# PEER mixer of a two-layer diffusion backbone: the order in which token tiles are ranked, and where the gathered expert rows are placed

## The chip, the cores and the metric

The kernel runs on one core of a Trainium2 chip. The metric is the device time of one execution in microseconds (us), the median of the runs. The core has five engines with a queue each: TensorE (PE), VectorE (DVE), ScalarE (ACT), GpSimd (POOL) and SyncE (SP). SP only issues DMAs here; POOL also issues the indirect DMAs that gather rows. Each engine takes its own queue strictly in order.

## The reference, cut to what matters

640 tokens of width 1024 (128 context tokens, 512 latent tokens) pass two layers. Each layer has a sequence mixer and then a channel mixer named PEER. In PEER every token picks 8 heads x 16 experts out of 16384, and each expert is one row of a table u and one row of a table v:

```python
q = (x @ wq).reshape(ntok, 8, 2, 128)
s = einsum('thpk,hpnk->thpn', q, keys)
sv, si = top_k(s, 16)                      # per head, per half of the key
cand = sv[:, :, 0, :, None] + sv[:, :, 1, None, :]
fv, fpos = top_k(cand, 16)                 # 16 of 256 sums
eidx = si0 * 128 + si1 at fpos             # 8 x 16 expert numbers for a token
g = softmax(fv)
act = gelu(einsum('td,ted->te', x, u_tab[eidx]))
out = einsum('te,ted->td', g * act, v_tab[eidx])
```

Everything is float32 at the interface. The two sequence mixers (S5 and RG-LRU in layer 0, Hyena in layer 1) are not touched by the change.

## The kernel before, in words

The 640 tokens are five tiles of 128 tokens. Tile 0 holds the context, tiles 1 to 4 the latents. `peer(l)` runs once in each layer and treats the tiles in two ways. Tiles 0 and 1 are **gathered**: for each of the 128 expert slots of a token, one indirect DMA issued by POOL (L1041) brings 128 rows of 1024 float32, 512 KB, into one of five buffers `gb`. DVE then either multiplies the row with the tokens and sums it (L1053, a "u row") or adds it to `acc` with its weight (L95, a "v row"). One such gather with its DVE operation is called a row below: 128 u rows and then 128 v rows for a tile, 512 rows in each layer, tile 1 first, then tile 0. Tiles 2 to 4 are **dense**: they are multiplied with all 16384 experts, and a gate matrix that holds `g` at the picked experts and zero elsewhere selects.

The stages of `peer(l)` in order of the program:

- Query stage (L1074 to L1122). `proj3` multiplies with `wq` in 16 steps m, two for each head, and `evq` forms the scores of all five tiles at L1101, in the order `ORD`. The first three tiles of `ORD` (slots s = 0, 1, 2 of `ef` and `gt`) are ranked at once: `top16` on DVE, then `stage2`, which sends sums and products to POOL and turns positions into expert numbers `ef`. For slots 1 and 2 (`DECA`) ACT sums the last product (L1014); for slot 0 POOL and DVE do (L1017, L1018). The scores of the fourth and the fifth tile are kept in `sc2` and `sc1`. After each head, `take(it0, BSLOT)` emits BSLOT rows of tile 1. With each m, `tick` emits a part of the matmuls that prepare the modulation vectors (L129).
- Two of the 128 dense up-projections are made ahead (L1149).
- Gate stage (L1362 to L1369). For n = 0, 1, 2, that is tiles 2, 3, 4, `gate_prep(n)` fetches `ef[:, ORD.index(NG + n)]`, and `gate` forms the gate matrix in 16 steps. Each step emits one row (`WSLOT`), whose DVE operation is ordered behind the last `OI` of the step (`behind`). Beside it `late(3, sc2)` ranks the fourth tile of `ORD`, a head for each pair of steps.
- Dense stage (L1254 to L1317 and L1380 to L1391). 128 iterations of 128 experts each: loads of u and v (512 KB each), splits into high and low parts on ACT and DVE, 24 matmuls of the up-projection (L1145), 18 of the down-projection (L1296), and between them gelu and gate. Every eighth iteration loads 1.5 MB of gate matrix `Gt` (L1262). In iterations 0 to 8 `late(4, sc1)` ranks the fifth tile of `ORD`. Rows are emitted as they fall due:

```python
nw = sum(WSLOT[i % len(WSLOT)] for i in range(16 * ND)) + 8 * BSLOT
...
due = min(4 * 128 - nw, (i + 1) * LRATE_N // LRATE_D)
take(it, due - done[0])
```

- Tail: `back` (layer 0) or `final` (layer 1) of the dense tiles, the rest of the rows, and `back` or `final` of tile 0, which needs the last row.

The text of the program is not the order of the queues. The program is built with a scheduler (`schedule_with_timeline_sim=True`) that simulates the instructions and fixes the order in each queue when the kernel is built. The trace shows that order.

The change touches three constants: `ORD` (L926), `BSLOT` (L934) and `LRATE_N` (L956). They act on `evq` (L1100, L1114), `gather` (L1045), `gate_prep` (L1188) and the loop at L1379 to L1391.

Of the kernel before, what the change touches and what calls it, by code (L numbers as in the profile page):

```python
# [43 lines left out]
def tile_kernel(ctx: ExitStack, tc: tile.TileContext, I, O, dbg=None, upto=99):  # L44
# [104 lines left out]
    def tick(n=1):  # L149
        for _ in range(n):  # L150
            if bgm[0] is None or next(bgm[0], False) is False:
                bgm[0] = None
                break
# [769 lines left out]
    g_d = [dram.tile([16, 128, TD // 16, 8, 16], F32, name=f"g_d{l}") for l in range(2)]  # L923

    FG0, FG1 = 6, 3
    ORD = (1, 2, 3, 4, 0)  # L926
    NGB = 5
    NGS = 3
    NRES = 4
# [1 line left out]
    DECH = 8  # L931
    CANDE = G
    WSLOT = (1,)
    BSLOT = 7  # L934
    MTICK = 1
    OIP = (0, 0, 0, 1)
    CT = ((10, 2), (10, 2))
# [15 lines left out]
    MQ = 4  # L953
    MODS_Q = [[(0, (10, 11)), (1, tuple(range(MQ)))], [(1, (10, 11))]]
    VSUB = (0,)
    LRATE_N, LRATE_D = 16, 4  # L956

    def peer(l):
        pool = ExitStack()
# [84 lines left out]
        def gather(i):  # L1044
            s0 = ORD.index(i)  # L1045
            ei = gp.tile([128, 128], I32, name="ei", tag="ei", bufs=2)
            act = gp.tile([128, 128], F32, name="act", tag="act")
            for s in range(128):
                if s % 16 == 0:
                    V.tensor_copy(ei[:, s:s + 16], ef[:, s0, s:s + 16])  # L1050
                b = rows(f"peer_u{l}", ei, s)
                with behind():
                    V.scalar_tensor_tensor(b, b, 1.0, hrow[:, i], op0=ALU.mult, op1=ALU.mult,  # L1053
                                           accum_out=act[:, s:s + 1])
                yield
            w = gp.tile([128, 128], F32, name="pw", tag="pw", bufs=2)
            S.activation(w, act, AF.Gelu_apprx_tanh)
            mul(w, w, gt[:, s0])
            acc = accs[i]
            for s in range(128):  # L1060
                b = rows(f"peer_v{l}", ei, s)
                if s == 0:
                    ts(acc, b, w[:, 0:1], None, ALU.mult, None)
                else:
                    stt(acc, b, w[:, s:s + 1], acc, ALU.mult, ALU.add)
                yield

        def take(it, n):
            for _ in range(n):
                next(it, None)  # L1070
# [3 lines left out]
        with ExitStack() as e0:  # L1074
# [19 lines left out]
            def evq(m, p):  # L1094
# [4 lines left out]
                pb = ps.tile([128, 2, 128], F32, name="psc2", tag="sm2")  # L1099
                for s, i in enumerate(ORD):  # L1100
                    PE.matmul(pa[:, s] if s < 3 else pb[:, s - 3], q[:, i * 128:(i + 1) * 128], keys[:, m],  # L1101
# [10 lines left out]
                if m % 2 == 1:  # L1112
                    stage2(qp, m // 2, 0, 3, v, iu, lambda sh, dt, n: qp.tile(sh, dt, name=n, tag=n, bufs=2))
                    take(it0, BSLOT)  # L1114
                tick(MTICK)
# [71 lines left out]
        def gate_prep(n):  # L1187
            s0 = ORD.index(NG + n)  # L1188
            cd = kp.tile([128, 11, 128], I32, name="cd", tag="Gs", bufs=NGS)
            e32, ij = cd[:, 0], cd[:, 1:3]  # L1190
            ab, fa = (cd[:, 3 + 4 * i:7 + 4 * i].rearrange("p (a b) c -> p a b c", b=2) for i in range(2))
            fa = fa.bitcast(F32)
            V.tensor_copy(e32, ef[:, s0])
            ts(ij[:, 0], e32, 7, None, ALU.logical_shift_right, None)
            ts(ij[:, 1], e32, 127, None, ALU.bitwise_and, None)
            ts(ab[:, 0], ij, 4, None, ALU.logical_shift_right, None)
            ts(ab[:, 1], ij, 15, None, ALU.bitwise_and, None)
            V.tensor_copy(fa, ab)
            ts(fa[:, 0], fa[:, 0], -4.0, None, ALU.add, None)
            ts(fa[:, 1], fa[:, 1], -8.0, None, ALU.add, None)  # L1200
            V.tensor_copy(code[:, 1:3], fa)
            mul(fa, fa, fa)
            stt(code[:, 0], fa[:, 0], -1.0, fa[:, 1], ALU.add, ALU.add)
            nc.sync.dma_start(c_d[l][n], code)
            cr = kp.tile([128, 4, 2, 128], BF16, name="cr", tag="cr", bufs=2)
            nc.sync.dma_start(cr, c_d[l][n].rearrange("(c t) r h k -> (t r) c h k", c=4))
            gT = kp.tile([128, 128], F32, name="gT", tag="gT", bufs=2)
            pt = ps.tile([128, 128], F32, name="pgT", tag="sm")
            PE.transpose(pt, gt[:, s0], ident)
            S.copy(gT, pt)  # L1210
            return cr, gT
# [163 lines left out]
        with ExitStack() as e3:  # L1375
            lp = e3.enter_context(tc.tile_pool(name=f"peerl{l}", bufs=1))
            acc = pp.tile([128, NG, D], F32, name="acc", tag="sc1")
            accs[:] = [acc[:, i] for i in range(NG)]
            nw = sum(WSLOT[i % len(WSLOT)] for i in range(16 * ND)) + 8 * BSLOT  # L1379
            for i, _ in enumerate(dense(lp)):  # L1380
# [366 lines left out]
```

## Time and profile before

| | us |
|---|---|
| median of 3 runs | 4148.82 |
| lowest and highest run | 4145.64, 4162.87 |
| profiled execution, its time | 4159.84 |
| profiled execution, its span | 4158.0 |
| busy in the span: PE, DVE | 3627.4 (87%), 3368.5 (81%) |
| busy in the span: POOL, ACT | 2269.1 (55%), 1708.3 (41%) |

The page of the profile gives busy time by engine, the span in 40 slices, the chain of work that ended last, and the costliest groups of instructions. The views named below are cut out of the same execution: busy time of each engine in chosen stretches, groups by line, waits, the chain in order of time, and the timeline. Times in a view are us from the span's start. A count stands behind an x.

### The profile page before, as it was taken

To read this page: it belongs to the slowest core of one execution; us is meant where nothing else is said; L and a number is where in the kernel's file an instruction comes from. 1 tells how busy PE (TensorE), PEld (TensorE's weight loads), DVE (VectorE), ACT (ScalarE), POOL (GpSimd) and SP (SyncE) were. 2 spreads that over 40 slices of the span, in tenths; PEclk is the share of its full clock that TensorE was granted. 3 is DMA by queue.
4 is the path that set the end of the run, shared out by engine and by line. 5 is a ranking of instruction groups with operands and counts; after the bars stand their busy time and mean duration, and the time that the engine had idled before them with its cause. 6 is when DMAs were issued, how large, how long until landed. Compare 5 with 4: busy or idle time off the path is not lost.

```text
span 4158.0 us, 57343 instructions
## 1 busy us (share of the span) xinstructions
PE 3627.4 (87%) x20098; PEld 3168.2 (76%) x20098; DVE 3368.5 (81%) x6122; ACT 1708.3 (41%) x3493; POOL 2269.1 (55%) x2046
## 2 busy tenths in 40 slices
PE   6867886588999999999689988843889999999996
PEld 4756873467899999999579778742678999999996
DVE  8873599889988887888865656998898888878889
ACT  3522334584333333333354333335843333333333
POOL 5641577658544444455655435886575444444455
PEclk9988998799999999999789999976999999999998
DMA  5565267398999999999724642653989999999997
GB/s 205 138 129 146 87 206 245 119 284 288 358 341 333 347 334 341 340 333 338 246 79 132 222 127 87 209 171 98 287 283 345 343 334 343 335 346 335 335 339 264
DMA packets 438105, 1057.42 MB, mean 254 GB/s; under 512 B 49175, under 2 KB 210967, under 8 KB 432696
## 3 DMA queue, kind: packets, MB, share of 16 engines
q0 software_dynamic: 152784, 555.55, 38.7%
q1 hardware_dynamic: 285032, 498.21, 35.4%
q8 instruction: 158, 2.59, 0.2%
q14 instruction: 131, 1.07, 0.1%
HBM read 993.86 MB, written 61.87 MB: 254 GB/s over the span
## 4 chain that ended last, share of the span: by engine, by line
PE 61%; DVE 22%; DMA 5%; issue 4%; ACT 4%; POOL 3%; SPq 1%; DVEq 0%; ACTq 0%; POOLq 0%
PE pA L1145 24%; PE pso L1296 23%; PE pproj L171 8%; DVE gb L1053 6%; PE pmod L129 1%; DVE oh L77 1%; DMA gb<-in_peer_u,ei 1%; PE pg L1245 1%; DVE OI L1240 1%; POOL gb L1041 1%; ACT Gs L1249 1%; DMA mw<-in_w_mod 1%; DVE tiu L977 1%; POOL jk L77 1%; DVE sc L978 1%
## 5 line engine op out<-in xcount | busy, mean ns | idle before, releaser
L1041 POOL DMA_INDIRECT gb<-in_peer_v,ei x512 | 679.3, 1327 | 627.8 <-DVE acc L95 550.9
L1041 POOL DMA_INDIRECT gb<-in_peer_u,ei x512 | 635.6, 1241 | 527.1 <-DVE gb L1053 401.9
L1296 PE MATMUL pso<-vh,wp 128*128 128x512 f32 x3072 | 874.1, 393 | 5.8 <-ACT wp L1285 4.2
L1053 DVE SCALAR_TENSOR_TENSOR gb<-gb,hrow 128x1024 f32<-128x1024 f32 x512 | 705.8, 1386 | 16.1 <-DMA gb<-in_peer_u,ei 16.1
L1145 PE MATMUL pA<-hHd,ul 128*128 128x384 f32 x2048 | 693.6, 339 | 27.8 <-DVE ul L77 27.8
L1145 PE MATMUL pA<-hHd,uh 128*128 128x384 f32 x2048 | 694.6, 339 | 15.3 <-DVE modT L77 6.7
L1145 PE MATMUL pA<-hLd,uh 128*128 128x384 f32 x2048 | 692.6, 338 | 0.0
L95 DVE SCALAR_TENSOR_TENSOR acc<-gb,pw,acc 128x1024 f32<-128x1024 f32 x508 | 662.0, 1303 | 21.4 <-DMA gb<-in_peer_v,ei 18.0
L1296 PEld LDWEIGHTS pso<-vh,wp 128*128 128x128 f32 x3072 | 574.9, 189 | 114.7 <-ACT wp L1285 5.4
L1137 ACT CAST uh<-wraw 128x1024 fp32r<-128x1024 f32 x256 | 269.2, 1051 | 664.3 <-PE pA L1145 664.2
L77 DVE TENSOR_TENSOR ul<-wraw,uh 128x1024 fp32r<-128x1024 f32 x256 | 318.6, 1244 | 212.1 <-ACT uh L1137 202.8
L1296 PE MATMUL pso<-vl,wp 128*128 128x512 f32 x1536 | 479.4, 393 | 7.5 <-DVE vl L77 7.4
L1145 PEld LDWEIGHTS pA<-hHd,ul 128*128 128x128 f32 x2048 | 389.1, 190 | 30.6 <-DVE ul L77 29.3
L1145 PEld LDWEIGHTS pA<-hHd,uh 128*128 128x128 f32 x2048 | 389.3, 190 | 27.1 <-ACT A L1146 6.9
L1145 PEld LDWEIGHTS pA<-hLd,uh 128*128 128x128 f32 x2048 | 389.1, 190 | 8.7
L1269 ACT CAST vh<-vraw 128x1024 fp32r<-128x1024 f32 x256 | 268.9, 1052 | 243.6 <-PE pso L1296 238.7
L77 DVE TENSOR_TENSOR vl<-vraw,vh 128x1024 fp32r<-128x1024 f32 x256 | 314.5, 1229 | 64.5 <-ACT vh L1269 51.8
L1296 PEld LDWEIGHTS pso<-vl,wp 128*128 128x128 f32 x1536 | 289.5, 189 | 73.6 <-DVE vl L77 9.5
L77 POOL TENSOR_TENSOR wl<-wraw,wh 128x1024 fp32r<-128x1024 f32 (+1 forms) x88 | 215.8, 2454 | 234.7 <-ACT wh L159 211.8
L1285 ACT CAST wp<-A 128x384 fp32r<-128x384 f32 x256 | 131.5, 514 | 428.6 <-DVE A L77 407.1
L1245 PEld LDWEIGHTS pg<-OI,OJ 128*128 128x128 f32 x1536 | 200.9, 202 | 99.7 <-POOL OI L77 34.2
L1245 PE MATMUL pg<-OI,OJ 128*128 128x128 f32 x1536 | 219.5, 292 | 40.9 <-POOL OI L77 16.0
(531 smaller groups left out, 6801.6 us busy)
## 6 DMA issues: line engine op xcount, KB each, us to landing
wraw<-in_uT SPq DMA_DIRECT2D x256, 512.0 KB
vraw<-in_peer_v SPq DMA_DIRECT2D x256, 512.0 KB
g_d<-Gs SPq DMA_DIRECT2D x48, 768.0 KB
Gt<-g_d SPq DMA_DIRECT2D x24, 1536.0 KB
wmod<-in_w_mod SPq DMA_DIRECT2D x48, 512.0 KB
wraw<-in_wq SPq DMA_DIRECT2D x32, 512.0 KB
mw<-in_w_mod SPq DMA_DIRECT2D x16, 1024.0 KB
wraw<-in_w_in_c SPq DMA_DIRECT2D x24, 512.0 KB
```

The source lines that it names most:

```text
L77: (eng or V).tensor_tensor(o, a, b, op=op)
L95: V.scalar_tensor_tensor(o, a, s, b, op0=op0, op1=op1)
L129: PE.matmul(pm[:2, :cw], cond[:, k], w[k], start=k == 0, stop=k == 7)
L171: PE.matmul(p[:, i, :sg[2]], a[:, k, :], sg[hl](k), start=k == 0 and a is wh and hl == 0, stop=k == kk - 1 and a is wl)
L1041: G.indirect_dma_start(out=b, out_offset=None, in_=I[tab], in_offset=bass.IndirectOffsetOnAxis(ap=ei[:, s:s + 1], axis=0))
L1053: V.scalar_tensor_tensor(b, b, 1.0, hrow[:, i], op0=ALU.mult, op1=ALU.mult, accum_out=act[:, s:s + 1])
L1137: S.copy(uh, u)
L1145: PE.matmul(pA, a[:, k], b[:, k], start=k == 0 and b is hHd and a is uh, stop=k == 7 and a is ul)
L1245: PE.matmul(pg[:, t], OJ[:, t4 * 4 + t], OI[:, t4 * 4 + t], start=True, stop=True)
L1269: S.copy(vh, v)
L1285: S.copy(WH, A)
L1296: PE.matmul(pso[n][h], a[:, c], b[:, h * 512:(h + 1) * 512], start=i == 0 and a is WH and b is vh, stop=i == 127 and a is WL)
```

## The change

Three constants differ. The ranking order becomes tiles 2, 3, 4, 1, 0: the three dense tiles are ranked in the query stage, tile 1 by `late(3, sc2)` in the gate stage, tile 0 by `late(4, sc1)` as before. The query stage emits no rows. The rows of the dense stage fall due at 15/4 for an iteration where 16/4 was used; as 48 rows are emitted before the dense stage (104 before the change), 464 are left for it (408 before the change), and they fall due over 124 of 128 iterations (102 before the change).

```diff
@@ -923,7 +923,7 @@
     FG0, FG1 = 6, 3
-    ORD = (1, 2, 3, 4, 0)
+    ORD = (2, 3, 4, 1, 0)
     NGB = 5
@@ -931,7 +931,7 @@
     WSLOT = (1,)
-    BSLOT = 7
+    BSLOT = 0
     MTICK = 1
@@ -953,7 +953,7 @@
     VSUB = (0,)
-    LRATE_N, LRATE_D = 16, 4
+    LRATE_N, LRATE_D = 15, 4
```

## Rows read from the trace of the kernel before

**Rows 1.** The chain that ended last, by line, whole span (page).
```profile
PE pA L1145 24%; PE pso L1296 23%; PE pproj L171 8%; DVE gb L1053 6%; PE pmod L129 1%; DVE oh L77 1%; DMA gb<-in_peer_u,ei 1%; PE pg L1245 1%; DVE OI L1240 1%; POOL gb L1041 1%; ACT Gs L1249 1%; DMA mw<-in_w_mod 1%; DVE tiu L977 1%; POOL jk L77 1%; DVE sc L978 1%
```
**Rows 2.** Busy time by stage: stretch, its length, busy us (count), clock, DMA.
```profile
core 0: us, PE busy (x) PEld busy (x) DVE busy (x) ACT busy (x) POOL busy (x), PEclk, DMA share, GB/s
474.00:780.00 306.00, 221.34 (x1224) 171.75 (x1224) 278.96 (x1040) 130.40 (x649) 220.38 (x272) 0.86 0.55 178
780.00:977.00 197.00, 161.98 (x1019) 127.71 (x1019) 172.72 (x420) 152.17 (x276) 137.29 (x170) 0.93 0.83 258
977.00:2030.00 1053.00, 1047.23 (x5264) 948.85 (x5262) 900.55 (x1095) 376.82 (x507) 547.14 (x421) 1.00 0.93 335
2030.00:2070.00 40.00, 5.83 (x30) 4.00 (x29) 34.27 (x26) 13.63 (x37) 32.54 (x24) 0.56 0.63 195
2553.00:2860.00 307.00, 185.59 (x1068) 162.19 (x1069) 277.51 (x1030) 126.69 (x640) 225.02 (x271) 0.78 0.47 148
...
500.00:520.00 20.00, 20.00 (x136) 18.22 (x135) 19.09 (x114) 8.95 (x42) 13.47 (x20) 1.00 0.13 45
```
**Rows 3.** Tails after the last L1296, 2030.3:2070 and 4120.4:4158: rows and their waiters.
```profile
L95 DVE SCALAR_TENSOR_TENSOR acc<-gb,pw,acc x18: 1271/1284/2932, 2029.6 to 2067.8; 128x1024 f32<-128x1024 f32 x18
...
  PE pac L1166: 27.2, 1
...
L95 DVE SCALAR_TENSOR_TENSOR acc<-gb,pw,acc x13: 1259/1273/2312, 4120.4 to 4145.0; 128x1024 f32<-128x1024 f32 x13
```
**Rows 4.** Gathers alone in parts of the dense stage: DVE busy (x), POOL busy (x).
```profile
1100.00:1800.00 700.00, 311.49 (x379) 325.50 (x251) 1.00 0.94 339
1800.00:2000.00 200.00, 102.45 (x80) 106.65 (x81) 1.00 0.95 337
```
**Rows 5.** Down-projection matmuls alone, L1296, same parts: PE busy (x), PEld busy (x).
```profile
1100.00:1800.00 700.00, 361.25 (x1515) 283.18 (x1513) 1.00 0.94 339
1800.00:2000.00 200.00, 102.98 (x432) 80.85 (x432) 1.00 0.95 337
```
**Rows 6.** Loads of the gate matrix, L1262, in layer 0: first and last issue.
```profile
L1262 SPq DMA_DIRECT2D Gt<-g_d x12: 332/334/892, 1019.3 to 1755.9; - x12
```
**Rows 7.** Rows in the query stage: DVE groups by line, layer 0 (474:780), then layer 1 (2540:2860).
```profile
L1053 DVE SCALAR_TENSOR_TENSOR gb<-gb,hrow 128x1024 f32<-128x1024 f32 x57 | 97.9, 1723 | 3.4 <-DMA gb<-in_peer_u,ei 3.4
...
L1050 DVE CAST ei<-ef 128x16 int32<-128x16 f32 x8 | 6.2, 774 | 0.0
...
L1053 DVE DVE_READ_ACCUMULATOR gb<-gb,hrow 128x1 f32 x57 | 4.3, 76 | 0.0
...
L1053 DVE SCALAR_TENSOR_TENSOR gb<-gb,hrow 128x1024 f32<-128x1024 f32 x56 | 94.2, 1688 | 3.3 <-DMA gb<-in_peer_u,ei 3.3
```
**Rows 8.** The u row by itself, over both layers: min/median/max ns.
```profile
L1053 DVE SCALAR_TENSOR_TENSOR gb<-gb,hrow x512: 1194/1218/7120, 525.5 to 3830.9; 128x1024 f32<-128x1024 f32 x171
```
**Rows 9.** Timeline of POOL, then DVE, 540.65 to 544.2: start, us, engine, operation.
```profile
540.66 2.41 POOL L77 TENSOR_TENSOR wl<-wraw,wh 128x1024 fp32r<-128x1024 f32 x1
...
540.79 3.37 DVE L1053 SCALAR_TENSOR_TENSOR gb<-gb,hrow 128x1024 f32<-128x1024 f32 x1
```
**Rows 10.** Waits, 640:780: who waited for whom, total, times, longest.
```profile
POOL jk L77 <- DVE gb L1053: 21.7, 2, 20.1
```
**Rows 11.** Chain in order of time, 2836:2862, end of layer 1's query stage.
```profile
2836.67 0.79 DVE ef L1018
2837.47 0.07 issue
2837.53 3.28 POOL jk L77 x2
2840.81 7.45 issue
2848.26 0.27 DVE code L1185
...
2858.25 1.01 PE pj L1225 x2
```
**Rows 12.** Timeline of POOL, then DVE, 4113 to 4119.5: gathers issued back to back.
```profile
4113.19 1.36 POOL L1041 DMA_INDIRECT gb<-in_peer_v,ei  x1 [0.30 <-issue]
...
4119.16 0.94 POOL L1041 DMA_INDIRECT gb<-in_peer_v,ei  x1 [0.30 <-issue]
...
4114.12 3.92 DVE L95 SCALAR_TENSOR_TENSOR acc<-gb,pw,acc 128x1024 f32<-128x1024 f32 x3
```
**Rows 13.** Busy time in the 5 us with the highest DMA rate seen, columns as in the stage view.
```profile
531.00:536.00 5.00, 3.79 (x27) 3.53 (x25) 4.69 (x9) 1.70 (x3) 4.70 (x3) 1.00 1.00 382
```

## The prediction, made from the trace of before

> **What bounds the kernel now.** I read the chain that ended last first. Its two largest lines are the dense matmuls, L1145 and L1296, and the u row on DVE (L1053) follows with 6% [rows 1]. So the limit changes from stage to stage, and the second view is busy time by stage [rows 2]. In the query stage of layer 0 (474 to 780) DVE is busy 279.0 of 306 us and PE 221.3 at a granted clock of 0.86; in layer 1 it is 277.5 against 185.6. DVE bounds this stage, and DMA is half idle (share 0.55). The gate stage (780 to 977) is mixed: no engine is over 88%. In the dense stage (977 to 2030) PE is busy 1047.2 of 1053 us at clock 1.00, DVE 900.6, and the DMA share is 0.93. PE bounds it, DMA is close behind, and DVE has some 150 us unused. The tail (2030 to 2070) has an idle PE, which waits 27.2 us in one piece for the last rows [rows 3].
>
> The third view is the pace of rows in the dense stage, and the argument hangs on it. From 1100 to 1800 there are 251 gathers [rows 4] and 1515 matmuls of L1296 [rows 5]; with 18 in an iteration these are 84.2 iterations of 8.3 us, so 2.98 rows for an iteration. From 1800 to 2000 it is 81 gathers in 24 iterations, 3.38. The program asked for 4. Rows therefore lag behind their due times: 18 v rows of layer 0 and 13 of layer 1 are left when the matmuls end [rows 3], though all had fallen due 26 iterations earlier. The order of the queues, fixed at build time, sets 3.0 to 3.4, not LRATE. The two paces differ by 0.40 rows, 0.2 MB, which is the 1.5 MB of Gt in every eighth iteration, and the last Gt load is issued at 1755.9 [rows 6]: the planned pace looks like an equal flow of DMA bytes. That is argued, not shown.
>
> **The change part by part.** I reckon for one layer; the layers are alike.
>
> *56 rows leave the query stage.* Rows there cost DVE 97.9 us in 57 pieces, and 94.2 in 56 in layer 1 [rows 7]. A u row by itself takes 1.218 us at the median [rows 8], so 56 are 68.2; the accumulator reads (4.3) and the index casts (6.2) make it 78.7, say 79. The other 27 us (97.9 minus 69.4, 94.2 minus 68.2) are waits inside the instruction: a row that began at 540.79 took 3.37 us, because a POOL subtraction that began at 540.66 ran 2.41; it ended 1.1 us after that one [rows 9]. The nearest rows do not show whether such a wait goes with the row or is taken over by the next DVE operation; ends 0 and 27, I take half, 13. Against the gain: rows filled every gap. Before the first of them, DVE was busy 19.09 of 20 us [rows 2], 5% idle; with more steps in flight I take 7% of the 171 us of DVE work that stays (279.0 minus 97.9, 4.3 and 6.2), minus 12, ends 8 and 20. POOL is rid of 56 gathers too, and of a queue in which a gather kept its product `jk` waiting for 20.1 us [rows 10]; that is inside the 79, not beside it. PE has 221 us of work in the stage at a low clock and ACT 130, so DVE stays the last one, narrowly.
>
> The Trainium skill bears on the half: "SBUF — State Buffer", section "Who interferes with whom", says that a VectorE instruction with two SBUF inputs and a GpSimd instruction that reads SBUF exclude each other for the whole instruction. The trace agrees in the 3.37 us above. By that rule the 27 us are a queue for POOL, whose work stays; all of it gone would make the total below some 27 us less, all of it taken over some 27 us more.
>
> *Dense tiles are ranked first.* Before, the gate of tile 2 read slot 1, whose expert numbers come last from ACT; now it reads slot 0, which DVE finishes. In layer 1 slot 0 ends at 2837.5, the code of the gate starts at 2848.3 and the first gate matmul at 2858.3 [rows 11]. ACT must still finish its sums before its first gate operation, so of these 11 us I take 9, ends 0 and 12. Tile 4 no longer needs the late ranking, which by the program is done in the first of the three gates while tile 4 is read in the third: nothing.
>
> *Tile 1 is ranked late.* A new wait: the first gather of the gate stage stands on POOL behind the index of head 0, and behind it on POOL are gate products and the ranking's own sums; DVE's row operation waits for the landing. The ranking work is the same as before, of another tile. 54 rows in 197 us are one in 3.6 us, and DVE has 24 us free in the stage [rows 2], which hides one late head. I take 0, ends 0 and 10.
>
> *LRATE 15/4.* 3.75 is above the 3.38 that the queues ever reached [rows 4, 5]. It costs and gains nothing; it would matter below 3.4.
>
> *56 rows arrive in the dense stage, and go through it.* About 55 rows are done when it begins, instead of 111. At an unchanged pace the same number is done in it, and so 18 + 56 = 74 rows are left in layer 0 and 69 in layer 1. Up to the last matmul nothing changes: PE stays at 8.3 us an iteration. The last u row of tile 0 moves 19 iterations (56 / 3.0) later, still before the buffer `hrow` is needed in the tail: nothing. In the tail a row costs what the slowest of its three steps takes. DVE: 3 rows in 3.92 us, 1.31 each. POOL: from 4113.19 to 4119.16 four gathers, 1.49 each [rows 12]. DMA: 0.524 MB at the 339 GB/s of the dense stage [rows 4] is 1.55, at the best 5 us (382 GB/s, [rows 13]) 1.37. I take 1.50: 84 us, ends 74 and 90. Layer 0's own tail shows 18 rows in 38.2 us, 2.25 with the last rows' start distance [rows 3], but with `back` and the norm on POOL among them; those are there once and not for each row.
>
> *Sum.* Query stage: 79 + 13 - 12 = 80, gate start 9, together -89 (ends -59 and -110). Tail: +84 (ends 74 and 90). That is -5 for a layer and -10 for both: 4158.0 becomes 4148, and with the 1.8 us around the span 4150. The profiled execution stands 11 us above the median of the runs; by the median I forecast 4139.
>
> So work is moved, not removed: from a stage bound by DVE, where a row costs some 1.6 us, to a tail in which nothing but rows runs, where it costs 1.5.
>
> **Rivals.** (a) *Rows fit into the dense stage.* DVE has 150 us free there and a row needs 1.34, so 56 more need 75. If the order at build time, with other neighbours, takes 3.5 rows an iteration, the tail stays as it is and the query gain remains: 4149 - 2 x 89, about 3975. For it speaks the idle DVE; against it that a pace of 4 was asked for and 3 was planned in 84 iterations, and a DMA share of 0.94. The Trainium skill ("DMA: Bandwidth & Descriptors", section "Specifications") gives 358 GB/s from HBM for a core; an estimate by it leaves room for 24 MB or 46 rows beside 335 GB/s in 1053 us, so (a) would keep 10 rows in the tail and lose some 15 us of its gain in each layer. The trace shows 382 GB/s for 5 us, above that figure, and no long stretch above it. (b) *The query stage does not shrink with DVE.* Projection, POOL's split of the weights, ranking and ACT's sums form a ring of small buffers; POOL is busy 220 us, 150 without its gathers. It decides if a head takes over 26 us where DVE's 171 / 8 is 21: then the gain with the gate's start is 45 and not 89, the tail still grows by 84, and the time is 4149 + 78 = 4227, slower. (c) *The tail runs at layer 0's 2.25 us for a row*: 126 - 89 = 37 for a layer, 4223, slower. (d) *The change does not do what it says*: rows are not spread over the dense stage by LRATE. That is part of my forecast, with its time.
>
> **How the numbers follow.** Forecast 0.72, (a) 0.11, (b) 0.10, (c) 0.07. The forecast's own ends are 4149 + 2 x (74 - 110) and 4149 + 2 x (90 + 10 - 59), 4077 to 4231; both extremes need all terms on one side, so 4090 to 4190 is its likely part. The range for 8 in 10 leaves out (a) and most of the far halves of (b) and (c): 4080 to 4215. 0.5% is 21 us, about what a measurement of this kernel can tell from no change. Of the forecast, about a third lies below 4128, half within, a sixth above 4170: faster 0.11 + 0.24 = 0.35, same 0.38, slower 0.17 + 0.10 = 0.27.
>
> **What would show it.** The query stages should be some 80 us shorter, with DVE still over 90% busy and no L1053 in them; the code of the first gate should follow slot 0's sum at once. In the dense stage L1296 should take 1053 us again, with 3.0 and then 3.4 gathers an iteration, and 65 to 75 rows should follow the last matmul in each layer, with PE idle for some 110 us. I am wrong if the pace in the dense stage is over 3.3 with Gt loads in it, if DVE falls under 85% in the query stage, or if rows in the tail are further apart than 1.7 us.

## The result: slower by 0.64%, and the profile after

The changed kernel takes 4176.78 us (median of 4 runs, 4171.53 to 4179.42), the kernel before 4147.77 beside it; the ratio is 1.0064, 95% interval 1.0049 to 1.0078. By the ratio that is 27 us more, by the two medians 29, where 10 less was forecast (4139). The time lies in the range, but on the other side of no change.

The profiled execution has a span of 4175.0. The first profile of before (4158.0) stood some 11 us above the median, so the stages are compared with a second one, of 4143.3. A stage ends where the next begins: query, from the first matmul with `wq` to the first of the gate (L1225); gate, to the first L1296; dense, to the last L1296; tail, to layer 1's first `wq` matmul (with layer 1's sequence mixer in it) or to the end of the span.

| us | before, layer 0 | after | | before, layer 1 | after | |
|---|---|---|---|---|---|---|
| query | 298.5 | 227.5 | -71.0 | 303.5 | 209.2 | -94.3 |
| gate | 198.4 | 196.8 | -1.6 | 203.9 | 200.1 | -3.8 |
| dense | 1054.7 | 1056.2 | +1.5 | 1055.0 | 1058.2 | +3.2 |
| tail | 520.4 | 623.0 | +102.6 | 37.5 | 132.1 | +94.6 |

Query and gate give -170.7, the dense stages +4.7, the tails +197.2, and the part ahead of the first stage +0.4: +32 between these two executions. So all that the query stages gain is lost again in the tails, and 26 us more.

The stages of after in the view that [rows 2] shows of before: stretch, its length, busy us (count) of PE, PEld (TensorE's loads of weights), DVE, ACT and POOL, granted clock, DMA share (mean busy share of the 16 DMA engines), GB/s.

```profile
472.00:700.00 228.00, 203.43 (x1209) 162.78 (x1210) 183.12 (x918) 127.27 (x648) 139.36 (x215) 0.95 0.35 108
700.00:896.00 196.00, 161.06 (x1017) 127.94 (x1031) 177.09 (x426) 153.80 (x279) 130.25 (x170) 0.92 0.82 257
896.00:1952.00 1056.00, 1048.30 (x5264) 949.50 (x5263) 895.20 (x1151) 378.23 (x507) 544.10 (x420) 1.00 0.92 335
1952.00:2102.00 150.00, 9.04 (x36) 5.40 (x35) 120.37 (x113) 20.86 (x46) 115.87 (x83) 0.52 0.76 252
2575.00:2785.00 210.00, 174.11 (x1065) 154.08 (x1065) 182.77 (x912) 125.48 (x640) 139.39 (x215) 0.91 0.26 77
4043.00:4175.00 132.00, 6.14 (x24) 4.57 (x24) 103.60 (x108) 8.58 (x16) 82.23 (x68) 0.51 0.80 280
```

In the query stages DVE is busy 183 us instead of 279 and 278, as the rows are gone. In the tails PE does next to nothing for 150 and 132 us. DVE is busy 80% and 78% of them, POOL 77% and 62%, and the transfers run at 252 and 280 GB/s: no engine and no transfer rate is full there. This is where the prediction failed.

The tails by line L95 (duration min/median/max in ns, first and last start; then who waited), layer 0 and layer 1. They answer to [rows 3].

```profile
L95 DVE SCALAR_TENSOR_TENSOR acc<-gb,pw,acc x75: 1269/1285/2674, 1951.9 to 2101.1; 128x1024 f32<-128x1024 f32 x75
...
  PE pac L1166: 88.4, 1
...
L95 DVE SCALAR_TENSOR_TENSOR acc<-gb,pw,acc x69: 1255/1285/2310, 4042.6 to 4163.3; 128x1024 f32<-128x1024 f32 x69
```

75 and 69 rows end after the last matmul instead of 18 and 13 (57 and 56 more), and `back` of tile 0 waits 88.4 us in one piece instead of 27.2. In layer 1, 56 rows more made the time from the last matmul to the last row 121.6 us instead of 25.8: 1.71 a row.

The waits in the steady part of layer 1's tail (4063 to 4150): who waited for whom, total, times, longest.

```profile
DVE acc L95 <- DMA gb<-in_peer_v,ei: 18.3, 22, 3.3
POOL gb L1041 <- DVE acc L95: 12.4, 12, 3.7
POOL gb L1041 <- issue: 9.4, 31, 0.3
POOL gb L1041 <- DMA gb<-in_peer_v,ei: 3.7, 6, 0.8
```

DVE waits for rows that have not landed, and POOL waits, before it issues a gather, for DVE to have read the row that lies in the buffer. Each waits for the other by way of the five buffers `gb`.

The pace of rows in the dense stage, two parts of layer 0, which answers to [rows 4, 5]: POOL with gathers alone, then PE and PEld with L1296 alone.

```profile
1020.00:1720.00 700.00, 326.91 (x251) 1.00 0.93 340
1720.00:1920.00 200.00, 106.64 (x80) 1.00 0.94 336
```

```profile
1020.00:1720.00 700.00, 361.72 (x1518) 283.97 (x1519) 1.00 0.93 340
1720.00:1920.00 200.00, 103.45 (x435) 81.17 (x435) 1.00 0.94 336
```

251 gathers in 1518 / 18 = 84.3 iterations are 2.98, and 80 in 24.2 are 3.31: the pace of before (2.98 and 3.38) but for 0.07 in the second part, with other rows.

The chain in order of time at the end of layer 1's query stage, which answers to [rows 11], and then of layer 0's:

```profile
2760.46 0.62 DVE oh L77
...
2765.16 4.55 ACT jk L1014 x32
...
2770.09 2.80 ACT jk L1014 x21
...
2772.91 1.56 ACT jk L1014 x11
...
2774.63 0.27 DVE code L1185
...
2784.67 0.58 PE pj L1225
```

```profile
646.91 5.98 DMA mw<-in_w_mod
...
652.93 5.30 PE pmod L129 x16
...
658.26 5.96 DMA mw<-in_w_mod
...
685.56 3.62 PE pmod L129 x16
689.18 0.27 PE pgT L1209
```

In layer 1 the code of the gate waits for ACT's last sums, which end 13 us after DVE's last operation of the ranking (`oh`). It was so in the kernel before, whose chain [rows 11] names no releaser for the 7.45 us ahead of the code at 2848.26. This is ACT's last sum there, which ends 0.2 us ahead of it:

```profile
2847.90 0.19 ACT L1014 ACTIVATION_READ_ACCUMULATOR jk<-jk 128x1 f32 x1
```

In layer 0 the last 46 us (643 to 689) are the matmuls of the modulation vectors and the loads of their weights in turn: without rows they end last. Layer 0's query stage is 18 us longer than layer 1's; the runs with `MTICK = 2` below took 9 of them away, and what the rest is stays open.

### The profile page after: what moved, and what is told of

Read it like the earlier page. It is cut to its first block, busy times and chain, and to the rows that moved or that the text cites. A ratio compares the mean times of both kernels' runs of the same rounds, so it can differ in the third digit from the quotient of the medians.

```text
span 4175.0 us, 57357 instructions
## 1 busy us (share of the span) xinstructions
PE 3593.2 (86%) x20066; PEld 3147.3 (75%) x20098; DVE 3315.3 (79%) x6122; ACT 1710.8 (41%) x3494; POOL 2246.4 (54%) x2046
## 4 chain that ended last, share of the span: by engine, by line
PE 62%; DVE 17%; DMA 7%; ACT 5%; issue 4%; POOL 4%; SPq 1%; POOLq 0%; DVEq 0%; ACTq 0%
PE pA L1145 24%; PE pso L1296 24%; PE pproj L171 8%; DMA gb<-in_peer_v,ei 2%; PE pmod L129 2%; DVE gb L1053 2%; POOL gb L1041 2%; ACT Gs L1249 1%; DVE OI L1240 1%; POOL jk L77 1%; DVE oh L77 1%; DMA gb<-in_peer_u,ei 1%; DVE sc L978 1%; ACT OJ L1226 1%; DVE tiu L977 1%
## 5 line engine op out<-in xcount | busy, mean ns | idle before, releaser
L1041 POOL DMA_INDIRECT gb<-in_peer_u,ei x512 | 658.2, 1286 | 566.0 <-DVE gb L1053 504.6
L1296 PE MATMUL pso<-vh,wp 128*128 128x512 f32 x3072 | 873.4, 393 | 1.1 <-ACT vh L1269 1.1
L95 DVE SCALAR_TENSOR_TENSOR acc<-gb,pw,acc 128x1024 f32<-128x1024 f32 x508 | 658.2, 1296 | 56.8 <-DMA gb<-in_peer_v,ei 52.0
L1296 PEld LDWEIGHTS pso<-vh,wp 128*128 128x128 f32 x3072 | 574.4, 188 | 108.6 <-ACT vh L1269 1.5
L1053 DVE SCALAR_TENSOR_TENSOR gb<-gb,hrow 128x1024 f32<-128x1024 f32 x512 | 642.7, 1266 | 13.7 <-DMA gb<-in_peer_u,ei 13.7
L1296 PE MATMUL pso<-vl,wp 128*128 128x512 f32 x1536 | 480.9, 393 | 9.8 <-DVE vl L77 9.7
L1296 PEld LDWEIGHTS pso<-vl,wp 128*128 128x128 f32 x1536 | 289.5, 189 | 75.9 <-DVE vl L77 11.4
```

Source lines behind the costliest of these rows:

```text
L95: V.scalar_tensor_tensor(o, a, s, b, op0=op0, op1=op1)
L1041: G.indirect_dma_start(out=b, out_offset=None, in_=I[tab], in_offset=bass.IndirectOffsetOnAxis(ap=ei[:, s:s + 1], axis=0))
L1296: PE.matmul(pso[n][h], a[:, c], b[:, h * 512:(h + 1) * 512], start=i == 0 and a is WH and b is vh, stop=i == 127 and a is WL)
```

## The experiments

### The kernel before once more

> The kernel before once more, for a second profiled execution of it: its first one stood 11 us above the median. Theory A (these 11 us lie in the query and gate stages, since those of the kernel with only the rank order changed came out 2.6 and 6.1 shorter without a better median): the query and gate stages of both layers together are 5 to 15 shorter than in the first profile, dense stages and tails within 3. Rival B (they lie elsewhere, or this execution has them too): query and gate stages within 4 of the first profile.

Measured: 4145.02, span 4143.3. Query and gate stages are together 9.0 us shorter than in the first profile, the dense stages and tails within 2.4 each, and 2.5 lie ahead of the first stage. Theory A holds for the larger part; this execution is the one that the table above compares with.

### How to read the rest

Ratios are to runs of the kernel before made beside it; a time without a ratio is one run. "After" is the changed kernel, and edits are against it unless said otherwise.

### The parts of the change, one at a time

**The rank order alone** (against the kernel before; 7 rows a head stay in the query stage):

```diff
-    ORD = (1, 2, 3, 4, 0)
+    ORD = (2, 1, 3, 4, 0)
```

> The kernel before with tile 2 in slot 0 and tile 1 in slot 1 (ORD = 2, 1, 3, 4, 0): the rank order's effect on the first gate alone, with the seven rows for each head still in the query stage, tile 1 ranked early, LRATE 16/4. Theory A (order is worth the few us by which the gate stage became shorter, 5.2 and 5.5): the stretch from the first gate matmul to the first L1296 falls by 3 to 9 in each layer, and the time is some 10 below the kernel before, ratio 0.9975 (0.996 to 0.9995). Rival B (the order itself, with more of the ranking in the wrong place, costs the time that the change lost): no gain or a loss, ratio 1.000 to 1.006. The tails stay at 18 and 13 rows by both.

Measured: 4148.80 us, ratio 0.9995 (0.9986 to 1.0004). Against the second profile of before, query and gate together are 3.5 us longer in layer 0 and 4.7 shorter in layer 1. The gate stage, which theory A wanted 3 to 9 shorter, is 3.8 and 0.4 longer, and the time is at the edge of both expectations: the order is worth nothing that can be measured.

**No rows in the query stage, and nothing else** (against the kernel before):

```diff
-    BSLOT = 7
+    BSLOT = 0
```

> The kernel before with BSLOT 0 alone: no rows in the query stage, tile 1 still ranked first, LRATE 16/4. Theory A (56 rows saved at 1.4 to 1.7 us in the query stage are paid back at 1.74 us in the tail; the order is worth some 5 us a layer): query stages some 80 and 95 shorter, 74 and 69 rows after the last matmul, tails 95 to 100 longer, no gain at the first gate; time some 10 above the changed kernel, 4187, ratio 1.009 (1.006 to 1.012). Rival B (ranking tile 1 late, or LRATE, is what cost the time): without them the time is at or below the kernel before, ratio 0.997 to 1.001.

Measured: 4176.35, ratio 1.0067 (1.0051 to 1.0082), the time of the whole change. Query and gate together are 66.1 and 100.6 us shorter, 74 and 69 rows are left. Rival B is out: BSLOT is the whole change. The chain at the end of layer 1's query stage, with tile 1 still in slot 0:

```profile
2762.40 7.29 ACT jk L1014 x53
...
2769.72 1.56 ACT jk L1014 x11
...
2771.44 0.27 DVE code L1185
```

ACT's sums end last here too, with the old order. So whether slot 0 or 1 holds the first dense tile makes no difference: in both, the code of the gate follows ACT.

**LRATE back to 16/4:**

> The changed kernel with LRATE 16/4 again. Theory A (the pace of rows is set in the order of the queues and lies below both rates): rows per iteration and the 74 and 68 rows after the last matmul are as in the changed kernel within 2, time 4177 within 6, ratio 1.0064 (1.005 to 1.008). Rival B (the lower rate holds rows back): some 8 to 20 rows fewer in each tail, time 4130 to 4155, ratio 0.996 to 1.002.

Measured: 4175.29, ratio 1.0066 (1.0050 to 1.0081); 3.00 rows an iteration from iteration 16 to 104 in both layers, as after (3.00 and 3.01), and 76 and 69 rows left. LRATE does nothing.

### What sets the pace in the dense stage

```diff
-                    nc.sync.dma_start(GT[:, (i + GPF) // 8 % NRES], g_d[l][(i + GPF) // 8])
+                    pass
```

> The changed kernel without the loads of Gt inside the dense loop (1.5 MB in every eighth iteration from the prefetch on); the gate matrix of the later iterations is then that of the first ones, and the output is not the reference's. All else is as it was. Theory A (the planned pace is an equal flow of DMA bytes): 3.0 rows an iteration become 3.4 from the start of the dense stage on, so some 49 rows are left after the last matmul where 74 and 68 were; at 1.74 us each the tails are some 43 and 35 shorter, time 4177 - 78 = 4100 (4085 to 4115). Rival C (the ring of five buffers or DVE sets the pace): 2.9 to 3.1 rows an iteration as before, and a time within 10 of the changed kernel, 4167 to 4187.

Measured: 4063.09. Gathers, then L1296, from 1100 to 1700:

```profile
1100.00:1700.00 600.00, 323.40 (x243) 1.00 0.94 339
```

```profile
1100.00:1700.00 600.00, 309.11 (x1297) 242.32 (x1296) 1.00 0.94 339
```

243 in 72.1 iterations are 3.37, at the same 339 GB/s, and an iteration is still 8.31 us. So theory A's pace is right for five buffers: where 1.5 MB in eight iterations are not loaded, rows take their place, byte for byte. Four buffers keep the pace too (216 gathers in 72.4 iterations, 2.98, in the kernel with four below); seven and eight raise it with the Gt loads in place, so bytes alone do not set it. How the two act together in the scheduler's order was not tried. The gain was larger than expected: 40 and 35 rows were left, fewer than the 49 that had been counted in the queues' order, and each of the 35 and 34 rows fewer shortened a tail by 1.6 us (56.2 and 54.5 us).

### What a row costs in the tail

The distance of rows after the last matmul is asked here: its mean was 1.63 us over the last 40 rows of layer 1's tail in the changed kernel. Three edits vary what can set it. The first:

```diff
-    NGB = 5
+    NGB = 4
```

> The changed kernel with four gather buffers gb instead of five. By the queues' order the dense stage keeps its pace of 3.0 and some 85 rows are left after the last matmul. What is asked is the distance of rows in the tail, 1.66 us in the changed kernel. T1 (the transfers' rate is the limit, 0.52 MB at some 316 GB/s): 1.6 to 1.75 still, tails some 20 to 25 longer for the 11 to 16 more rows, time 4215 to 4230. T2 (the ring of buffers is the limit: one buffer is taken for 5 x 1.66 = 8.3 us from gather to sum): 8.3 / 4 = 2.07, tails some 55 longer, time 4270 to 4300. T3 (DVE and POOL keep each other waiting): as T1.

The second leaves the adds out where s is 64 or more in tile 0:

```diff
                 b = rows(f"peer_v{l}", ei, s)
+                if i == 0 and s >= 64:
+                    yield
+                    continue
```

> The changed kernel, in which the last 64 v rows of tile 0 are gathered but not added (the adds are left out, so the output is not the reference's). What is asked is the distance of gathers on POOL after the last matmul, where a buffer comes free with its landing and DVE does not touch the rows. T1 (rate of the transfers): 1.6 to 1.7 us as with the adds, at some 316 GB/s. T2 (the ring of five): a buffer is taken for some 6 us and not 8.3, so 1.2 to 1.35, at 390 to 430 GB/s. T3 (DVE's adds slow POOL's issue or the landing): 1.2 to 1.3 and no waits for buffers.

The third opens three buffers more in the pool of the dense stage (`xtra`) and uses them in turn with the five. It needs room, which comes from one Gt buffer fewer (`NRES`); with that, layer 1's `final` of tile 1 and the rows that it multiplies with are made later (`FROW`, `F0`). A control has that room without the buffers. Four lines are not shown: `xtra` and `nrow` start empty, `xtra[0]` becomes the pool of the dense stage, and the rows for `final` that lie in a Gt buffer move to another one.

```diff
-    NRES = 4
+    NRES = 3
...
-    FROW = 110
-    F0 = 120
+    FROW = 121
+    F0 = 123
...
-            b = gp.tile([128, D], F32, name="gb", tag="gb", bufs=NGB)
+            nrow[0] += 1
+            if xtra[0] is not None and nrow[0] > 432 and nrow[0] % 8 >= 5:
+                b = xtra[0].tile([128, D], F32, name="gb", tag="gx", bufs=3)
+            else:
+                b = gp.tile([128, D], F32, name="gb", tag="gb", bufs=NGB)
```

> The changed kernel with eight gather buffers for the last 80 rows alone, five before that; the room comes from one Gt buffer fewer and a slightly smaller working set. Some 85 rows are left after the last matmul by the queues' order. T1 (rate): rows in the tail 1.6 to 1.7 us apart still, each landing later behind its issue (7 us or more instead of 4.6), time 4210 to 4225. T2 (ring): 1.3 to 1.45 apart, DVE's 1.31 or POOL's issue next in line, at 370 to 400 GB/s, time 4165 to 4185. T3 (DVE and POOL): 1.6 to 1.7 with the landing as before.

> The changed kernel with one Gt buffer fewer and the smaller working set that make room for eight buffers, but with five: what the room itself costs. By the queues' order 85 to 87 rows are left after the last matmul instead of 68 to 74. Theory: 28 to 30 rows more at 1.7 us, time 4215 to 4235, rows in the steady part of the tail 1.6 to 1.7 us apart as with the full room. Against the theory: below 4190, which would make the room a gain by itself.

Rows alone (tile `gb`) in the steady part of layer 1's tail: stretch, DVE busy (adds), POOL busy (gathers), clock, DMA share, GB/s. After, with five buffers:

```profile
4070.00:4150.00 80.00, 60.68 (x48) 54.88 (x47) 0.50 0.90 318
```

four buffers:

```profile
4100.00:4190.00 90.00, 60.58 (x49) 58.77 (x48) 0.50 0.82 278
```

eight for the last 80 rows:

```profile
4060.00:4120.00 60.00, 56.62 (x45) 46.57 (x44) 0.50 1.01 397
```

gathers without adds:

```profile
4030.00:4090.00 60.00, 0.00 (x0) 41.93 (x45) 0.50 1.03 411
```

and the control with five buffers in the smaller room:

```profile
4070.00:4150.00 80.00, 61.54 (x48) 61.58 (x48) 0.50 0.88 309
```

The waits in the same stretches, with four buffers and then with eight, to be set beside the 18.3 and 12.4 us of five above:

```profile
DVE acc L95 <- DMA gb<-in_peer_v,ei: 31.4, 42, 2.2
POOL gb L1041 <- DVE acc L95: 20.0, 20, 2.6
```

```profile
DVE acc L95 <- DMA gb<-in_peer_v,ei: 1.9, 3, 0.9
POOL gb L1047 <- DVE acc L95: 0.6, 1, 0.6
```

With four buffers a row comes every 1.86 us, with five every 1.67, with eight every 1.33, and then DVE is busy 94% of the time, the rate is 397 GB/s, and both waits are all but gone. Gathers alone come every 1.33 too, at 411 GB/s. So T1 and T3 fall: neither the rate nor DVE's adds hold the rows at 1.67. The ring does, as T2 says. What holds them at 1.33 with eight buffers was not separated: the DMA share is 1.01 there too.

T2's size for four buffers (2.07) was too large, since the 8.3 us are no constant. Over the last 40 rows of layer 1 a buffer was taken for 7.3 us with five buffers, from the start of its gather to the end of its add, and 0.8 went by until the next gather into it started: 8.1 in all, a fifth of which is 1.63. With four it was 6.9 and 0.6, with eight 9.5 and 1.1. The time with four buffers, 4223.78, fell into the band that T1 gave, but by another way: 79 and 73 rows were left and not 85, each dearer.

The times: 4156.02 with eight buffers in the tail, 4180.57 for the control, 4110.90 for the gathers without adds, one run each. Eight buffers came out 9 us better than T2 said, and the control 35 us better than expected, because 78 and 74 rows were left in it and not 85 to 87. The room alone costs some 4 us by that, which is less than two runs of one kernel can differ by (the seven of the kernel before beside the control lie within 13.5 us); three buffers more, for 80 rows, give 25 back.

### Where the rows could go instead

Eight buffers in the whole dense stage, after the change and before it (the edit above without `nrow[0] > 432`):

> The changed kernel with eight gather buffers in the whole dense stage (the room comes from one Gt buffer fewer and a slightly smaller working set). By the queues' order 3.8 rows an iteration are then issued, and no row is left after the last matmul. That is 3.8 x 0.524 + 1.05 + 0.19 = 3.2 MB in 8.3 us, 389 GB/s, where the dense stage ran at 335 to 340 so far and gathers alone at 397 to 409. T2 (the ring of buffers was the limit, of the plan in the dense stage and of the chip in the tail): the dense stage stays at 1053 to 1075, both tails lose their 150 and 122 us of rows but some 10 to 20, time 3925 to 3975, ratio 0.945 to 0.96. Rival (the transfers cannot go above 340 beside the loads): 398 MB of the dense stage take 1170 us, and the time is 4130 to 4170.

> The kernel before with the same eight buffers: 56 rows in the query stage, tile 1 ranked first, LRATE 16/4. By the queues' order 3.9 rows an iteration, done some 20 iterations before the end. Theory A (a row of the query stage costs 1.4 to 1.7 us there; in a dense stage that has room it costs nothing): query and gate stages as in the kernel before, the tails lose their 18 and 13 rows, time 4080 to 4105; the change is then worth -130 to -160, where with five buffers it costs 27. Rival (the gain of eight buffers is in the tail alone and the query rows are as cheap): within 40 of the changed kernel with eight buffers.

Measured: 4126.64 after the change, ratio 0.9944 (0.9926 to 0.9963), and 4287.92 before it, ratio 1.0331 (1.0311 to 1.0351). After the change, with eight buffers, 3.95 rows go through an iteration and none is left at the end; but an iteration grows from 8.31 to 9.3 and 9.1 us, and the dense stages to 1151 and 1143 (after) and to 1149 and 1143 (before). So T2's time is missed by 150 us. The rival of the first expectation came close in its numbers (1170 us, 4130 to 4170), but its reason, a limit of 340 GB/s, does not hold, as the rates below show; the time before the change lies 183 us above theory A's band and far from the rival's. Two parts of the dense stages with eight buffers, after the change, in the view by stage, and what PE waited for from 1100 to 1600:

```profile
1100.00:1800.00 700.00, 641.14 (x3168) 567.02 (x3167) 608.24 (x729) 224.36 (x303) 428.08 (x298) 1.00 0.95 356
3400.00:3900.00 500.00, 465.22 (x2306) 411.61 (x2305) 438.90 (x568) 163.03 (x221) 306.32 (x220) 1.00 0.98 368
```

```profile
PE pA L1151 <- ACT A L1152: 19.8, 16, 1.7
PE pso L1302 <- ACT vh L1275: 17.4, 13, 1.9
PE pso L1302 <- DVE vl L77: 1.9, 3, 1.1
```

PE is no longer full (92% and 93%). All 39 us that it stands idle from 1100 to 1600 are these waits, nearly all for ACT; no engine waits for the landing of a load there. What the comparison was made for is plain all the same: with eight buffers the change is worth 4126.64 - 4287.92 = -161 us, with five +27. Its sign depends on the place to which the rows go. Against the kernel before as it was, with five buffers, the change with eight gains only 0.6%, since the eight buffers by themselves made the kernel before 3.3% slower.

Seven buffers in the dense stage and eight for the last 80 rows:

> The changed kernel with seven gather buffers in the dense stage and eight for the last 80 rows (room as in the kernels with eight). By the queues' order 3.4 rows an iteration, some 35 rows left after the last matmul. Theory D (a dense iteration is stretched only where its transfers pass some 357 GB/s, the rate of the stage with eight buffers): 3.4 x 0.524 + 1.25 = 3.03 MB, 8.5 us an iteration and not 9.3; the dense stages 1055 to 1080, tails some 50 us of rows at 1.32 each, time 4045 to 4085, ratio 0.975 to 0.985, below the kernel before, the change and eight buffers. Theory E (every row above 3.0 an iteration costs the dense stage 1.0 us, as 3.94 rows made 8.31 us 9.29): 8.7 us an iteration, dense stages about 1105, time 4115 to 4140.

Here the buffer is chosen by the row's number modulo seven up to row 432, and modulo eight behind it. Measured: 4072.17, ratio 0.9816 (0.9800 to 0.9833). Of the kernels that leave nothing out it is the fastest, 105 us below the changed one.

```profile
1100.00:1800.00 700.00, 677.12 (x3361) 607.78 (x3360) 596.32 (x733) 240.82 (x322) 358.60 (x279) 0.99 0.94 351
3400.00:3900.00 500.00, 479.94 (x2407) 432.36 (x2407) 427.51 (x560) 171.31 (x229) 260.95 (x203) 1.00 0.94 354
```

3.48 rows an iteration, 18 and 24 left. Iterations take 8.88 and 8.69 us, so the dense stages are 1107 and 1092: the time is that of theory D, the length of the iteration that of theory E. In the second half of the dense stages most pairs of iterations take 16.6 us, as at 3.0 rows, and one pair in four, at or just behind a Gt load, takes 18.6 to 20.6. That looks like a limit of the transfers, but the waits speak against it: PE's 23 idle us from 1100 to 1800 are waits for ACT (20.1 for `vh`, 1.3 for `A`) and DVE (1.2), no engine waits for the landing of a load, and the kernel before moved 396 GB/s from 1055 to 1115 with PE busy 59.8 of 60 us. So the order of the queues is the likelier cause; no run tested it. The kernel before with seven buffers was not run, so how much of the 1.8% is the change and how much the buffers stays open.

The same with `MTICK = 2`, and eight buffers with it:

> The same with MTICK 2 (the modulation vectors' matmuls are emitted twice as fast in the query stage). With eight buffers MTICK 2 took 9 us from layer 0's query stage and 1 from layer 1's. Theory: some 8 us below the kernel with seven and eight buffers, query stage of layer 0 at 218. Against it: within 3 or slower.

> The changed kernel with eight buffers and MTICK 2: the matmuls of the modulation vectors are emitted twice as fast in the query stage. In the changed kernel the query stage of layer 0 ends with 46 us in which TensorE makes only these matmuls and waits for their weights, and takes 228 us where layer 1 takes 210. Theory (without rows in it the stage of layer 0 is bound by them): layer 0's query stage 10 to 20 shorter, layer 1's within 4, time 10 to 20 below the kernel with eight buffers and MTICK 1. Rival (they take the place of the projection, whose weights and scores then come later): within 5 or slower.

Measured: 4077.11 (ratio 0.9829, 0.9813 to 0.9846) beside 4072.17, and 4118.19 (0.9928, 0.9906 to 0.9949) beside 4126.64. Layer 0's query stage became 8.5 and 9.2 us shorter, so its end was bound by the modulation matmuls as read. With seven buffers layer 1's query stage grew by 4 and its dense stage by 18, and nothing of the gain comes out at the end. With eight the median fell by 8.5, less than the 10 to 20 expected, and as the intervals of the pair overlap it is not clear of noise.

## Why the prediction was wrong, point by point

**The query stage: the sum was right, its parts were not.** Forecast -80 a layer for the rows; BSLOT alone gave -66 and -101, a mean of -83.3 with the gate stage, so the mean hides two layers that were taken to be alike. DVE's busy time was to fall by 92 and fell by 95.8 and 94.7, by errors that largely cancel. The accumulator reads (4.3) lie inside the time of their row operation (one from 526.64 to 526.72 in an operation from 525.49 to 526.72), so they were counted twice, and 1.9 of the index casts' 6.2 us stayed. On the other side I had let half of the waits inside L1053 go, and they went whole: DVE's operations other than L1053 and L1050 are busy 181.9 us in layer 0's query stage with the rows and 181.6 without, 185.0 and 180.7 in layer 1, where half of the waits would have added some 13. DVE's idle time was to grow by 12; it grew by 18 in layer 0 and fell by 2 in layer 1. DVE is busy 80% of the stage in layer 0, below the 85% that I had named as a sign of error, and rightly: there the modulation matmuls end last, which no rival had. It is busy 87% in layer 1. The "over 90%" was a slip of its own: 187 busy in 226 us, as the sum had it, are 83%.

**The gate's start: wrong.** 9 us a layer were forecast. [rows 11] shows 7.45 us without a releaser behind slot 0's last product, and I gave most of it to the order. It is the rest of ACT's sums, which end at 2848.1, just ahead of the code, and end last in the new order too; the order gave nothing (ratio 0.9995, and 1.0064 beside 1.0067). The text had named that ACT must finish, and then priced it at 2 of 11 us.

**Tile 1 late, LRATE: right**, at nothing. **The dense stage: right.** The pace is as before and 75 and 69 rows are left (74 and 69 forecast). That the planned pace is an equal flow of bytes, argued then, is borne out by the kernel without Gt loads, but for five buffers only: with eight, 3.95 rows go through an iteration.

**The tail: the step that failed.** The price of a row was taken as the slowest of three steps, 1.50 us. The slowest was a fourth thing that the sum did not have, the ring of five buffers: a buffer goes round from the start of its gather by way of DVE's read to the start of the next gather into it in 8.1 us over the last 40 rows of layer 1, and a fifth of that is the distance of rows, 1.63 (1.67 from 4070 to 4150, 1.71 over the added rows of layer 1). The three steps that I priced were fast enough: with eight buffers they run at 1.33, so DVE's 1.31 was right and POOL's 1.49 and DMA's 1.37 to 1.55 [rows 12, 13] were too high. Beside that, 57 more rows cost layer 0 102.6 us, 8 more than the 56 of layer 1; `back` and the norm on DVE and POOL lie among them there, and what of it they cost was not tried. Together the tails came out 197 us longer and not 168, which is 1.75 for each of the 113 rows added, where 1.50 was forecast. Between the profiles the forecast was off by 42 us (-10 against +32): the tails are 29 of them, the query and gate stages together 7 (the gate's start, less the somewhat larger gain of the rows), the dense stages 5.

**Rival (a)**, that the rows fit into the dense stage, was given 0.11, by engines and rates alone. It was right that engines and rates leave room for more rows there: what kept them out was the number of buffers. But it was too hopeful in that they cost nothing: the stage itself grows, by 51 and 34 us at 3.48 rows an iteration and by 95 and 85 at 3.95. **Rival (c)** had the right sign: the measured 2.25 us of layer 0's own tail were set aside for a price put together from single steps, and the truth lay between the two.

The trace of the kernel before was read wrongly for rival (a): 382 GB/s over 5 us [rows 13] is not its highest rate, and it has stretches above 358. It moved 425 GB/s from 9 to 29 and 396 from 1055 to 1115, loads and gathers mixed:

```profile
1055.00:1115.00 60.00, 59.77 (x300) 53.76 (x299) 54.16 (x55) 21.75 (x30) 35.26 (x26) 1.00 1.02 396
```

The Trainium skill ("DMA: Bandwidth & Descriptors", section "Specifications") was drawn on for 358 GB/s. Gathers without adds moved 411 GB/s over 60 us, so that figure is no cap for one core alone. The skill says so itself in "Perfetto Trace Analysis", section "Roofline": a core that runs alone can go beyond its share, up to some 435 GB/s of its 16 DMA engines. The runs agree with that, and show 356 to 368 in the dense stage with eight buffers, where plain loads and gathers are mixed.

## What to carry to other kernels

Where work is moved into a stretch that nothing else fills, price it by the loop it runs in and not by its engines: the time from the issue of a transfer by way of the last read of its buffer to the next issue into it, divided by the number of buffers, is a bound of its own, and the first to look at when no engine and no rate is full. Moving work from one bound stage to another gave nothing here; with room where it goes the same move gained 3.8% (eight buffers before and after) where it had cost 0.6% (five). But the room had a price of its own, 3.3% on the kernel before: compare with the kernel that you have, against which the best mix here gained 1.8%. And where the chain shows an idle stretch without a releaser, look for an engine whose work ends just ahead of the next step, as ACT's did here, before the stretch is credited to the change.

## What the runs showed of the hardware beyond this

Gathers of 512 KB reach 397 GB/s with their adds and 411 without, each over 60 us; loads and gathers mixed reached 396 in the kernel before. A gather landed 4.7 us after its instruction on POOL had ended with five buffers, 4.3 with four and 5.2 with eight (means of the last 20 of layer 1). The executions with five buffers lie between 4.3 and 4.9 over both layers, so the step from four to five is not clear; five buffers without adds, where rows come as fast as with eight, land at 5.2 as well. So a gather lands later the more of them are under way, and a ring gains less than its number of buffers says.
